# Layer 1 MLP: VectorE's low halves one item behind ScalarE's high halves, no weight items between two pairs of feature tiles

## The chip, the cores and the metric

The kernel runs on one core of one Trainium2 chip. The metric is the device time of one execution in microseconds (us); less is better. TensorE (PE) multiplies, VectorE (DVE) and ScalarE (ACT) work element by element, GpSimd (POOL) helps them, SyncE (SP) issues the DMA transfers. Each engine works through its own queue in program order and waits where an operand isn't ready.

## The reference, cut to what matters

Two layers of a diffusion backbone on 512 latent and 128 context tokens, with 1024 features, all in 32-bit floating point. Each layer ends with an MLP of 4096 hidden features:

```
def squared_relu_mlp(h, w1, w2):
    a = jax.nn.relu(h @ w1)
    return (a * a) @ w2

h = rms_norm(x, norm2_g[l]) * (1 + sc2) + sh2
x = x + g2 * squared_relu_mlp(h, w_ff1[l], w_ff2[l])
```

The change is in the MLP of layer 1, the last large stage before the final norm.

## The kernel before, in words

**High and low halves.** Every matrix operand is kept as two parts: a high half, the value rounded to TensorE's fast 32-bit format (fp32r), and a low half, the value minus its high half. One product is made of three matmuls (`mm3`, L805 to L810): high times high, high times low, low times high. The high half is written by ScalarE (a copy), the low half by VectorE (a subtraction that reads the high half). So the two engines hand each item on to each other.

**The weight queue.** `Weights` holds a list of items in the order of their use. `loads` (L176) issues their DMAs into five raw buffers of 128 x 1024 values, as far as these are free. `pump` (L195) processes the next item: ScalarE writes the high half (L216), VectorE the low half (L225), and `used` (L244) gives the raw buffer back, which lets the next load be issued. If no weight slot is free, `pump` does nothing. `need` (L255) pumps until an item is there. The calls of `pump` stand between the matmul groups and so fix the order of the work on ScalarE and VectorE. Some other items (the modulation's, L457) release code a counted number of items later (`flush`, L248).

**Up projection with seven products.** Layer 1's hidden features come in eight blocks of 512 (four feature tiles of 128). Blocks 0 and 1 are computed in the ordinary way ahead of `blocks7` (L1644). From block 2 on, `up7` (L1562) computes two feature tiles f and g for both token chunks of 320 (0 and 1) at once, with seven products instead of eight (a Strassen-like scheme). A block has two such pairs, p = 0 and 1. The seven weight operands of a pair (items `w1s`, 0 to 6) are combinations of four quarters f0, g0, f1, g1 of the raw weights. `w1s_use` (L555) writes the high half of an item (L565, 128 x 512), its low half (L566), and for items 0, 1, 2 and 4 a follow-up (L570) that overwrites a quarter in place; the follow-up of item 0 is read by item 1, that of 1 by 2, that of 2 by 3, that of 4 by 5.

Within a pair the products run in the order 0 to 6, each 12 matmuls. ScalarE copies the result of product 0 to p1 (L1615). VectorE makes u2 = p1 + product 2 and u3 = u2 + product 1 (L1620, L1621, traced at L1593 in `add`). Product 4 adds into the bank that product 1 left and u3 has read; products 5 and 6 likewise add into the banks of products 3 and 0. Sums with u2 and u3 give the hidden features of (g, 1), (g, 0) and (f, 1); (f, 0) comes straight from the last bank. `finish` (L1595) squares the positive part (ScalarE: Relu L1603, Square L1604; for (f, 0) Relu L1600 and a multiplication by VectorE, L1601), writes the high half (ScalarE, L1605) and returns the low half (VectorE, L1606), which is issued a product later.

**Down projection.** After a block's two pairs come its 16 down tiles (8 feature tiles x 2 chunks, 12 matmuls each), each followed by a residual update on VectorE (L1414) and, from the third tile on, one call of `pump`. The first four tiles start with half of their products. The four down weights of a block (items `w2`, 128 x 1024) are queued behind its 14 `w1s` items. Behind the last tile stands one `pump(2)` (L1670). So, in the steady state, the first pair's weights and item 0 of the second pair are processed in the down tiles, items 1 and 2 of the second pair between the blocks, items 3 to 6 and the first down weight in the first pair, the other three down weights in the second pair. While blocks 0 and 1 are multiplied down, VectorE and ScalarE also make the sums of activations that the seven products need (`sums`, L1516).

The last block (7) goes through its down tiles in two wider chunks of tokens (384 and 256), without any call of `pump`.

Of the kernel before, what the change touches and what calls it, by code (L numbers as in the profile page):

```python
# [136 lines left out]
class Weights:  # L137
# [3 lines left out]
    def __init__(self, nc, raw):  # L141
        self.nc, self.raw = nc, raw
        self.items, self.loaded, self.done = [], 0, 0
        self.raw_live, self.raw_cap, self.tiles, self.of = 0, RAWB, {}, {}
        self.raws = {}
        self.slots = None
        self.caps = {}

        self.lo = nc.vector
        self.own = {}  # L150
        self.hold = None
        self.slow = ()
        self.later, self.skip = [], False
        self.keep, self.second = {}, None

    def add(self, key, loads, size, use=None):
        self.items.append((key, loads, size, use))
# [37 lines left out]
    def pump(self, n=1):  # L195

        if self.skip:
            self.skip = False
            return
        while n > 0 and self.done < len(self.items):  # L200
            key, loads, size, use = self.items[self.done]
            own = self.own.get(key)
            if (use is None or key[0] == "w1s") and own is None and self.full(key) or key == self.hold:
                return
            self.loads()
            if self.done not in self.raws:
                return
            ts = self.raws.pop(self.done)
            if use is None:
                if own is None:  # L210
                    self.of[key], w = self.slots.take([128, 2, 1024], F32R)
                else:
                    w = own()
                r = ts[0][:, 0:size]
                hi, lo = w[:, 0, 0:size], w[:, 1, 0:size]
                self.nc.scalar.activation(out=hi, in_=r, func=AF.Copy)  # L216
                eng = self.nc.gpsimd if key[0] in self.slow else self.lo
                if eng is None:
                    self.nc.scalar.activation(out=lo, in_=hi.bitcast(F32), func=AF.Copy, scale=-1.0)
                    src, shape = loads[0]  # L220
                    if len(shape) == 2:
                        lo = lo.rearrange("p (k n) -> p k n", k=shape[0])
                    self.nc.gpsimd.dma_start(out=lo, in_=src, accum_op=ALU.add)
                else:
                    eng.tensor_tensor(out=lo, in0=r, in1=hi.bitcast(F32), op=ALU.subtract)  # L225
                self.tiles[key] = w
                rest = None
            else:
                rest = use(ts)
            self.done += 1  # L230
            for f in self.later:
                f[0] -= 1
            self.flush(0)
            if rest:

                self.skip = False
                d = self.done
                self.pump()
                rest()
                self.skip = self.done > d  # L240
            self.used(self.keep.pop(key, len(loads)))
            n -= 1

    def used(self, n):  # L244
        self.raw_live -= n
# [9 lines left out]
    def need(self, key):  # L255
        while key not in self.tiles:
            self.skip = False
            d = self.done
            self.pump(1)
            assert self.done > d, (key, self.items[self.done][0])  # L260
        return self.tiles[key]

    def free(self, key):
# [12 lines left out]
def body(ctx, tc, a):  # L276
# [278 lines left out]
    def w1s_use(l, b, p, i):  # L555


        def use(ts):
            if i == 0:
                fast[l, b, p] = ts  # L560
            ab, cd = (t.rearrange("p (k n) -> p k n", k=4) for t in fast[l, b, p])
            f0, g0, f1, g1 = ab[:, :, 0:128], ab[:, :, 128:256], cd[:, :, 0:128], cd[:, :, 128:256]
            src = (f0, g0, g0, f0, g1, g0, f1)[i]
            w = st.half(("w1s", l, b, p, i)).rearrange("p a (k n) -> p a k n", k=4)
            act(out=w[:, 0], in_=src, func=AF.Copy)  # L565
            vec.tensor_tensor(out=w[:, 1], in0=src, in1=w[:, 0].bitcast(F32), op=ALU.subtract)  # L566
            todo = {0: (g0, f0, g0, ALU.subtract), 1: (g0, g1, g0, ALU.subtract), 2: (f0, g0, f0, ALU.add),
                    4: (g0, f1, g0, ALU.subtract)}.get(i)
            if todo:
                vec.tensor_tensor(out=todo[0], in0=todo[1], in1=todo[2], op=todo[3])  # L570

        return use

# [880 lines left out]
    def mlp(l, C, H, lead, CL, per_d, per_c, mid, tick=None, turn=None, seven=False):  # L1454
# [107 lines left out]
        def up7(b, p):  # L1562
            n = C[0][1]

            gone = []

            def product(i, op, ps, first):
                w = st.need(("w1s", l, b, p, i))
                if ps is None:
                    ps = bank("up_ps", n)  # L1570
                for k in range(4):
                    r = B[op, k] if isinstance(op, int) else H[op[0]][4 * op[1] + k]
                    mm3(
                        ps, (w[:, 0, tok(k)], w[:, 1, tok(k)]), (r[:, 0, 0:n], r[:, 1, 0:n]),
                        first and k == 0, k == 3, not first,
                    )

                gone.append(("w1s", l, b, p, i))
                if i:
                    st.free(gone.pop(0))  # L1580
                return ps

            f, g = 2 * p, 2 * p + 1
            rs = {}
            for j in (f, g):
                A[b, j] = fa.tile([128, 2, T], F32R, tag="aa", name="aa")
                rs[j] = fr.tile([128, 2, HW], F32, tag="r", name="r").rearrange("p a n -> p (a n)")

            def new(nm):
                return sc.tile([128, 328], F32, tag="n", name=nm)[:, 0:n]  # L1590

            def add(out, v, ps):
                vec.tensor_tensor(out=out, in0=v, in1=ps, op=ALU.add)  # L1593

            def finish(j, ci, src=None):  # L1595

                c = slice(*C[ci])
                r, aa = rs[j][:, c], A[b, j]
                if src is not None:
                    act(out=r, in_=src, func=AF.Relu)  # L1600
                    vec.tensor_tensor(out=r, in0=r, in1=src, op=ALU.mult)  # L1601
                else:
                    act(out=r, in_=r, func=AF.Relu)  # L1603
                    act(out=r, in_=r, func=AF.Square)  # L1604
                act(out=aa[:, 0, c], in_=r, func=AF.Copy)  # L1605
                return lambda: vec.tensor_tensor(  # L1606
                    out=aa[:, 1, c], in0=r, in1=aa[:, 0, c].bitcast(F32), op=ALU.subtract
                )

            def out(j, ci):  # L1610
                return rs[j][:, C[ci][0]:C[ci][1]]

            pa = product(0, (0, 0), None, True)
            p1 = new("p1")
            act(out=p1, in_=pa, func=AF.Copy)  # L1615
            st.pump()
            pd = product(1, 2, None, True)
            pb = product(2, 1, None, True)
            u2, u3 = new("u2"), new("u3")
            add(u2, p1, pb)  # L1620
            add(u3, u2, pd)  # L1621
            st.pump()
            pc = product(3, 0, None, True)
            add(out(g, 1), u3, pc)
            lo = finish(g, 1)
            st.pump()
            pd = product(4, 3, pd, False)
            add(out(g, 0), u2, pd)
            lo()
            lo = finish(g, 0)  # L1630
            if not p:
                st.pump()
            pc = product(5, (1, 1), pc, False)
            add(out(f, 1), u2, pc)
            lo()
            lo = finish(f, 1)
            if not p:
                st.pump()
            pa = product(6, (0, 1), pa, False)
            lo()  # L1640
            finish(f, 0, pa)()
            st.free(gone.pop(0))

        def blocks7(f0):  # L1644

            for b in range(NFB):
                if b >= f0:
                    for p in range(FB // 2):
# [7 lines left out]
                if b < NFB - 1:  # L1656
# [10 lines left out]
                    free(1)  # L1667
                    if b == f0 - 1:
                        bg.drain()
                    st.pump(2)  # L1670
                    continue
                for c in CL:
                    early = cut(range(3), CL[0:1]) if c is CL[0] else []
                    for d in range(KD):
                        if d < len(early):
                            ps = down(b, d, c, early[d][2], True, (3, 2))
                        else:
                            ps = down(b, d, c)
                        residual(ps, d, c, modc[l, 5])
                        per_d(c, d)  # L1680
                    per_c(c)
# [522 lines left out]
```

## Time and profile before

| what | before |
|---|---|
| time, median of 3 runs | 1323.13 us (1322.59 to 1324.24) |
| the profiled execution | 1321.14 us |
| its span, first to last instruction | 1319.2 us |
| mean granted TensorE clock | 0.978 |
| instructions | 20782 |
| busy: PE, DVE, ACT, POOL | 96%, 62%, 42%, 16% of the span |
| HBM read, written | 144.21 MB, 5.39 MB |

The page of the profile gives the busy time of each engine and the costliest groups of instructions. The view of waits says which instruction stood still for which other one. The timeline gives the instructions of an engine with their start and length, and in brackets the idle time before one and what ended it. The view of windows gives busy times and the granted TensorE clock in chosen stretches. "Low" and "high" are used below for the two halves of an item, "follow-up" for the subtraction at L570.

### The profile page before, as it was taken

The page shows a single profiled execution, that of the slowest core. Times are in us where ns is not written, and L with a number is a line of the kernel's source. Part 1 is how long each engine was busy: PE and PEld are TensorE (multiplying, and loading weights), DVE is VectorE, ACT ScalarE, POOL GpSimd, SP SyncE. Part 2 cuts the span into 40 slices and gives each one's busy share as a digit, 9 for nine tenths or more (in the row PEclk, how much of TensorE's full clock was granted, in tenths as well). Part 3 has the DMA queues.
Part 4 walks back from the last instruction along what each step waited for, and adds up shares of the span by engine and source line. Part 5 has one row for each costly group of instructions (what it writes and reads, how often), then busy time and mean ns, then how long its engine had stood idle before and what let it go on. Part 6 is the DMA issues. An engine that isn't in the chain of part 4 may idle for free.

```text
span 1319.2 us, 20782 instructions
## 1 busy us (share of the span) xinstructions
PE 1266.0 (96%) x8308; PEld 1193.5 (90%) x8308; DVE 823.2 (62%) x1565; ACT 551.4 (42%) x989; POOL 206.7 (16%) x182
## 2 busy tenths in 40 slices
PE   7999999999999999999999999899989898998987
PEld 5899875689999999999999998889989898998987
DVE  5753864554766666665666546767867566565654
ACT  3445454543553434333343425543242434334243
POOL 0010322212022222222222233300000000000001
PEclk8999899999999999999999998999989999999999
DMA  7742297250344444444343606503121312222102
GB/s 279 264 163 77 80 231 252 97 192 1 130 129 144 128 160 123 149 128 141 119 157 123 214 17 145 111 17 111 34 88 41 96 49 80 81 80 89 40 32 80
DMA packets 65376, 154.09 MB, mean 117 GB/s; under 512 B 5200, under 2 KB 22096, under 8 KB 64768
## 3 DMA queue, kind: packets, MB, share of 16 engines
q1 hardware_dynamic: 61360, 142.53, 32.9%
q0 software_dynamic: 3632, 10.16, 3.7%
q8 instruction: 65, 1.06, 0.3%
q14 instruction: 31, 0.25, 0.1%
q10 hardware_dynamic: 288, 0.08, 0.0%
HBM read 144.21 MB, written 5.39 MB: 113 GB/s over the span
## 4 chain that ended last, share of the span: by engine, by line
PE 75%; DVE 14%; ACT 7%; issue 2%; DMA 1%; POOL 0%; DVEq 0%; ACTq 0%; POOLq 0%
PE dn_ps L809 10%; PE dn_ps L808 10%; PE dn_ps L810 10%; PE up_ps L808 8%; PE up_ps L810 7%; PE up_ps L809 7%; ACT w L216 2%; DVE w L225 2%; DVE w L566 2%; DVE x L1414 2%; PE o_ps L1309 1%; PE wo_ps L808 1%; PE wo_ps L809 1%; PE wo_ps L810 1%; PE mod_ps L351 1%
## 5 line engine op out<-in xcount | busy, mean ns | idle before, releaser
L808 PE MATMUL dn_ps<-aa,w 128*128 128x320 f32 (+4 forms) x1024 | 317.8, 310 | 0.0
L809 PE MATMUL dn_ps<-aa,w 128*128 128x320 f32 (+4 forms) x1024 | 317.2, 310 | 0.0
L810 PE MATMUL dn_ps<-aa,w 128*128 128x320 f32 (+4 forms) x1024 | 316.4, 309 | 0.0
L809 PE MATMUL up_ps<-h,w 128*128 128x320 f32 (+2 forms) x800 | 249.0, 311 | 4.6 <-DVE h L759 4.6
L808 PE MATMUL up_ps<-h,w 128*128 128x320 f32 (+2 forms) x800 | 251.0, 314 | 1.3 <-ACT h L755 1.3
L810 PE MATMUL up_ps<-h,w 128*128 128x320 f32 (+2 forms) x800 | 249.4, 312 | 0.0
L1414 DVE SCALAR_TENSOR_TENSOR x<-dn_ps,mod,x 128x328 f32<-128x328 f32 (+5 forms) x360 | 145.0, 434 | 114.5 <-PE dn_ps L810 113.6
L225 DVE TENSOR_TENSOR w<-raw,w 128x1024 fp32r<-128x1024 f32 (+4 forms) x122 | 151.8, 1250 | 86.5 <-ACT w L216 85.4
L808 PEld LDWEIGHTS dn_ps<-aa,w 128*128 128x128 f32 x1024 | 192.6, 188 | 1.8 <-issue 0.8
L809 PEld LDWEIGHTS dn_ps<-aa,w 128*128 128x128 f32 x1024 | 192.5, 188 | 0.1
L810 PEld LDWEIGHTS dn_ps<-aa,w 128*128 128x128 f32 x1024 | 192.6, 188 | 0.0
L216 ACT ACTIVATE w<-raw 128x1024 fp32r<-128x1024 f32 (+4 forms) x131 | 132.7, 1026 | 114.1 <-DMA raw<-w_ff 86.9
L809 PEld LDWEIGHTS up_ps<-h,w 128*128 128x128 f32 x800 | 152.4, 191 | 5.4 <-DVE h L759 5.4
L808 PEld LDWEIGHTS up_ps<-h,w 128*128 128x128 f32 x800 | 152.7, 191 | 4.9 <-issue 3.4
L810 PEld LDWEIGHTS up_ps<-h,w 128*128 128x128 f32 x800 | 151.8, 190 | 0.0
L473 POOL TENSOR_TENSOR acc<-acc,raw 128x1024 f32<-128x1024 f32 x42 | 100.7, 2399 | 303.7 <-ACT raw L471 297.6
L565 ACT ACTIVATE w<-raw 128x512 fp32r<-128x512 f32 x84 | 50.9, 624 | 120.7 <-DVE raw L570 70.1
L566 DVE TENSOR_TENSOR w<-raw,w 128x512 fp32r<-128x512 f32 x84 | 57.8, 688 | 40.2 <-ACT w L565 39.6
L471 ACT ACTIVATE raw<-raw,cs 128x1024 f32<-128x1024 f32 x42 | 48.3, 1149 | 62.3 <-DVE acc L466 53.9
L1942 POOL TENSOR_TENSOR y<-y,fg 128x1024 f32<-128x1024 f32 x1 | 2.4, 2389 | 439.4 <-ACT y L1938 439.4
L1488 DVE TENSOR_TENSOR r<-r,up_ps 128x328 f32<-128x328 f32 (+2 forms) x80 | 37.4, 484 | 41.3 <-ACT r L1487 39.7
L1491 DVE TENSOR_TENSOR aa<-r,aa 128x640 fp32r<-128x640 f32 (+3 forms) x52 | 39.8, 766 | 35.6 <-ACT aa L1490 35.6
(407 smaller groups left out, 2134.3 us busy)
## 6 DMA issues: line engine op xcount, KB each, us to landing
raw<-w_ff SPq DMA_DIRECT2D x126, 512.0 KB, 3.7
raw<-w_mod SPq DMA_DIRECT2D x80, 512.0 KB, 3.9
raw<-w_m SPq DMA_DIRECT2D x16, 512.0 KB, 6.2
raw<-w_out SPq DMA_DIRECT2D x8, 512.0 KB, 4.3
w<-w_ff POOLq DMA_DIRECT2D x8, 512.0 KB, 10.0
kT<-ckvT POOLq DMA_DIRECT2D x4, 768.0 KB, 11.1
xr<-x SPq DMA_DIRECT2D x5, 512.0 KB, 5.6
xs<-x SPq DMA_DIRECT2D x2, 1280.0 KB, 8.9
```

The costliest lines, as they stand in the source:

```text
L216: self.nc.scalar.activation(out=hi, in_=r, func=AF.Copy)
L225: eng.tensor_tensor(out=lo, in0=r, in1=hi.bitcast(F32), op=ALU.subtract)
L471: act(out=raw if k else acc[1], in_=raw, func=AF.Copy, scale=w[1])
L473: nc.gpsimd.tensor_tensor(out=acc[1], in0=acc[1], in1=raw, op=ALU.add)
L565: act(out=w[:, 0], in_=src, func=AF.Copy)
L566: vec.tensor_tensor(out=w[:, 1], in0=src, in1=w[:, 0].bitcast(F32), op=ALU.subtract)
L808: mm(ps, lhsT=st_[0], rhs=mv[0], start=first, stop=False, skip_group_check=on)
L809: mm(ps, lhsT=st_[0], rhs=mv[1], start=False, stop=False, skip_group_check=on)
L810: mm(ps, lhsT=st_[1], rhs=mv[0], start=False, stop=last, skip_group_check=on)
L1414: vec.scalar_tensor_tensor(out=xv, in0=ps[:, p0:p0 + c1 - c0], scalar=gate[:, d, m:m + 1], in1=xv, op0=ALU.mult, op1=ALU.add)
L1488: vec.tensor_tensor(out=rv, in0=rv, in1=ps, op=ALU.mult)
L1491: vec.tensor_tensor(out=aa[:, 1, lo:hi], in0=r[:, lo:hi], in1=aa[:, 0, lo:hi].bitcast(F32), op=ALU.subtract)
```

## The change

There are four edits.

1. `Weights` gets a list `lag` and a flag `lagging`. The low half of an item (for `w1s` with its follow-up) and the return of its raw buffer are put on the list instead of being issued at once. Without the flag the list is emptied at the end of the same item; with the flag (set at the start of `blocks7`) it is emptied when the next item is about to be processed, or when the item itself is needed. In both cases the released code of `flush` now stands ahead of the low half.
2. In `up7` the first call of `pump` moves from behind product 0 to behind product 1, and the one behind product 4 is now made in both pairs.
3. `finish` becomes `high` (Relu, Square and the high half, all on ScalarE, also for (f, 0)) and `low`. The sum of a chunk is issued ahead of the high half of the chunk before it, and the low halves come one product later or at the end of the pair.
4. The `pump(2)` behind a block's down tiles is taken out, and the last block's down tiles get one call of `pump` each.

```
     def pump(self, n=1):
...
         while n > 0 and self.done < len(self.items):
+            self.lows()
             key, loads, size, use = self.items[self.done]
...
-                    eng.tensor_tensor(out=lo, in0=r, in1=hi.bitcast(F32), op=ALU.subtract)
+                    self.lag.append(
+                        lambda: eng.tensor_tensor(out=lo, in0=r, in1=hi.bitcast(F32), op=ALU.subtract)
+                    )
...
-            self.used(self.keep.pop(key, len(loads)))
+            n_raw = self.keep.pop(key, len(loads))
+            self.lag.append(lambda: self.used(n_raw))
+            if not self.lagging:
+                self.lows()
             n -= 1
+
+    def lows(self):
+
+        todo, self.lag = self.lag, []
+        for f in todo:
+            f()
...
     def need(self, key):
...
+            self.lows()
+        if self.lag and key == self.items[self.done - 1][0]:
+            self.lows()
         return self.tiles[key]
...
             act(out=w[:, 0], in_=src, func=AF.Copy)
-            vec.tensor_tensor(out=w[:, 1], in0=src, in1=w[:, 0].bitcast(F32), op=ALU.subtract)
             todo = {0: (g0, f0, g0, ALU.subtract), 1: (g0, g1, g0, ALU.subtract), 2: (f0, g0, f0, ALU.add),
                     4: (g0, f1, g0, ALU.subtract)}.get(i)
-            if todo:
-                vec.tensor_tensor(out=todo[0], in0=todo[1], in1=todo[2], op=todo[3])
+
+            def lows():
+                vec.tensor_tensor(out=w[:, 1], in0=src, in1=w[:, 0].bitcast(F32), op=ALU.subtract)
+                if todo:
+                    vec.tensor_tensor(out=todo[0], in0=todo[1], in1=todo[2], op=todo[3])
+
+            st.lag.append(lows)
...
-            def finish(j, ci, src=None):
-
+            def high(j, ci, src=None):
                 c = slice(*C[ci])
-                r, aa = rs[j][:, c], A[b, j]
-                if src is not None:
-                    act(out=r, in_=src, func=AF.Relu)
-                    vec.tensor_tensor(out=r, in0=r, in1=src, op=ALU.mult)
-                else:
-                    act(out=r, in_=r, func=AF.Relu)
-                    act(out=r, in_=r, func=AF.Square)
-                act(out=aa[:, 0, c], in_=r, func=AF.Copy)
-                return lambda: vec.tensor_tensor(
-                    out=aa[:, 1, c], in0=r, in1=aa[:, 0, c].bitcast(F32), op=ALU.subtract
-                )
+                r = rs[j][:, c]
+                act(out=r, in_=r if src is None else src, func=AF.Relu)
+                act(out=r, in_=r, func=AF.Square)
+                act(out=A[b, j][:, 0, c], in_=r, func=AF.Copy)
+
+            def low(j, ci):
+                c = slice(*C[ci])
+                hi, lo = (A[b, j][:, i, c] for i in range(2))
+                vec.tensor_tensor(out=lo, in0=rs[j][:, c], in1=hi.bitcast(F32), op=ALU.subtract)
...
             act(out=p1, in_=pa, func=AF.Copy)
+            pd = product(1, 2, None, True)
             st.pump()
-            pd = product(1, 2, None, True)
             pb = product(2, 1, None, True)
...
             pc = product(3, 0, None, True)
             add(out(g, 1), u3, pc)
-            lo = finish(g, 1)
             st.pump()
             pd = product(4, 3, pd, False)
             add(out(g, 0), u2, pd)
-            lo()
-            lo = finish(g, 0)
-            if not p:
-                st.pump()
+            high(g, 1)
+            st.pump()
             pc = product(5, (1, 1), pc, False)
+            low(g, 1)
             add(out(f, 1), u2, pc)
-            lo()
-            lo = finish(f, 1)
+            high(g, 0)
             if not p:
                 st.pump()
             pa = product(6, (0, 1), pa, False)
-            lo()
-            finish(f, 0, pa)()
+            low(g, 0)
+            high(f, 1)
+            high(f, 0, pa)
+            low(f, 1)
+            low(f, 0)
...
         def blocks7(f0):
 
+            st.lagging = True
             for b in range(NFB):
...
                         bg.drain()
-                    st.pump(2)
                     continue
...
                             ps = down(b, d, c)
+                        st.pump()
                         residual(ps, d, c, modc[l, 5])
                         per_d(c, d)
```

More of the change, by code (lines that the diff above doesn't have):

```diff
@@ L154, in __init__ @@
         self.keep, self.second = {}, None
+        self.lag, self.lagging = [], False
     def add(self, key, loads, size, use=None):
```

## The prediction

> **What bounds the kernel now.** I read the page first.
>
> ```profile
> span 1319.2 us, 20782 instructions
> ...
> PE 1266.0 (96%) x8308; PEld 1193.5 (90%) x8308; DVE 823.2 (62%) x1565; ACT 551.4 (42%) x989; POOL 206.7 (16%) x182
> ```
>
> TensorE works nearly all the time, so only what makes it stand still or run slowly is worth anything. The change acts from the layer 1 blocks on (about 898 us to 1282 us), so next came the view of waits from 925 to 1285 us.
>
> ```profile
> ACT w L565 <- DVE raw L570: 70.1, 33, 4.7
> ...
> DVE w L566 <- ACT w L565: 39.6, 45, 2.1
> DVE x L1414 <- PE dn_ps L810: 35.9, 51, 1.2
> DVE w L225 <- ACT w L216: 32.2, 18, 2.5
> PE up_ps L808 <- DVE u L1593: 23.2, 7, 4.0
> ```
>
> Columns: total us, times, longest. The last row is the only one that costs time: TensorE waits seven times for the sums u2 and u3. The others show why VectorE is late: it waits for ScalarE's copies and ScalarE for VectorE's results, in turn, each with little of its own queued meanwhile.
>
> Two rows of TensorE's timeline place the wait: always the fifth product (index 4) of a block's second pair, because it adds into the bank that u3 must first have read.
>
> ```profile
> 1038.71 0.51 PE L808 MATMUL up_ps<-w 128*128 128x320 f32 x1 [3.49 <-DVE u L1593]
> ...
> 1096.78 0.56 PE L808 MATMUL up_ps<-w 128*128 128x320 f32 x1 [3.49 <-DVE u L1593]
> ```
>
> They are 58.07 us apart, one block. The view of windows shows a second price behind such a wait (columns: window, length, busy us and instructions of PE, PEld, DVE, ACT, POOL, granted clock, DMA share, GB/s).
>
> ```profile
> 1020.00:1023.00 3.00, 3.00 (x22) 3.00 (x21) 2.39 (x5) 1.06 (x2) 0.00 (x0) 1.00 0.00 0
> ...
> 1038.70:1041.95 3.25, 3.24 (x12) 3.25 (x13) 1.40 (x2) 1.75 (x4) 0.00 (x0) 0.52 0.78 214
> ...
> 982.20:985.00 2.80, 2.80 (x19) 2.80 (x20) 1.37 (x2) 1.34 (x4) 0.00 (x0) 1.00 0.73 206
> ```
>
> After the 3.49 us wait the clock is 0.52 for 3.25 us: 3.25 x 0.48 = 1.56 us lost. The window at 982.20 follows the shortest of the seven waits (in the first layer-1 block of the seven-product form) and has clock 1.00. That wait is 23.2 - 4.0 - 5 x 3.49 = 1.7 us long.
>
> **What can be won.** The rows below are VectorE's timeline, from the end of one block through the next one's first pair into its second.
>
> ```profile
> 1012.36 0.68 DVE L1414 SCALAR_TENSOR_TENSOR x<-dn_ps,mod,x 128x192 f32<-128x192 f32 x2 [1.21 <-PE dn_ps L810]
> 1014.12 0.55 DVE L1414 SCALAR_TENSOR_TENSOR x<-dn_ps,mod,x 128x320 f32<-128x320 f32 x1 [1.08 <-PE dn_ps L810]
> 1015.88 0.68 DVE L1414 SCALAR_TENSOR_TENSOR x<-dn_ps,mod,x 128x192 f32<-128x192 f32 x2 [1.21 <-PE dn_ps L810]
> ...
> 1022.10 0.68 DVE L566 TENSOR_TENSOR w<-raw,w 128x512 fp32r<-128x512 f32 x1
> 1022.70 0.68 DVE L570 TENSOR_TENSOR raw<-raw 128x512 f32<-128x512 f32 x1
> ...
> 1034.13 0.48 DVE L1601 TENSOR_TENSOR r<-r,up_ps 128x320 f32<-128x320 f32 x1
> 1035.15 0.49 DVE L1606 TENSOR_TENSOR aa<-r,aa 128x320 fp32r<-128x320 f32 x1 [0.54 <-ACT aa L1605]
> 1036.42 1.23 DVE L225 TENSOR_TENSOR w<-raw,w 128x1024 fp32r<-128x1024 f32 x1 [0.78 <-ACT w L216]
> 1037.57 0.48 DVE L1593 TENSOR_TENSOR u<-p,up_ps 128x320 f32<-128x320 f32 x1
> 1038.08 0.49 DVE L1593 TENSOR_TENSOR u<-u,up_ps 128x320 f32<-128x320 f32 x1
> 1038.48 1.22 DVE L225 TENSOR_TENSOR w<-raw,w 128x1024 fp32r<-128x1024 f32 x1
> ```
>
> Each residual waits for TensorE, so 12 matmuls (one product, one down tile) take 1.76 us. A block is 14 products and 16 down tiles: 30 x 1.76 = 52.8 us. It takes 58.07, so 5.27 us are lost: the 3.49, the 1.56 and some 0.2 of pipeline refill. Five blocks: 5 x 5.27 = 26.4. The first block of the form loses 4.0 + 1.7 + 1.56 + 2 x 0.2 = 7.7. Together 34.1 us: all that this change can win.
>
> **Moving the lows and the adds: the new schedule of a pair.** ScalarE's rows for the same stretch:
>
> ```profile
> 1017.92 0.63 ACT L565 ACTIVATE w<-raw 128x512 fp32r<-128x512 f32 x1 [2.28 <-DVE raw L570]
> 1018.45 0.42 ACT L1615 ACTIVATE p<-up_ps 128x320 f32<-128x320 f32 x1
> ...
> 1030.63 0.47 ACT L1604 ACTIVATE r<-r 128x320 f32<-128x320 f32 x1
> 1031.14 0.47 ACT L1605 ACTIVATE aa<-r 128x320 fp32r<-128x320 f32 x1
> 1031.51 1.04 ACT L216 ACTIVATE w<-raw 128x1024 fp32r<-128x1024 f32 x1
> 1032.46 0.41 ACT L1600 ACTIVATE r<-up_ps 128x320 f32<-128x320 f32 x1
> 1034.65 0.47 ACT L1605 ACTIVATE aa<-r 128x320 fp32r<-128x320 f32 x1 [1.77 <-DVE r L1601]
> 1035.03 0.42 ACT L1615 ACTIVATE p<-up_ps 128x320 f32<-128x320 f32 x1
> 1035.34 1.99 ACT L216 ACTIVATE w<-raw 128x1024 fp32r<-128x1024 f32 x2
> ```
>
> Paces read from both fences: on VectorE the next instruction starts 0.60 us after a 512-wide one, 0.40 after a 320-wide one, 0.51 if it needs the one before; on ScalarE a 512-wide high takes 0.53 to the next start, three dependent 320-wide steps 1.48 in all; a hand-over between the engines costs 0.03 to 0.04 (1034.61 to 1034.65, 1035.12 to 1035.15). Zero is the last residual's start (1015.88), so product k of the first pair is readable at 1.76(k+1). TensorE wants product 4 of the second pair at 11 x 1.76 less the 0.2 by which it runs ahead of readers: 19.16. Before, u3 ended at 1038.57, which is 22.69; 3.5 late, as the waits say, so the clock of this sum is right.
>
> Following the new program order (the first pair now processes weight items 1 to 5 of the second, none in the gap before it):
> - VectorE does u2 at 5.28, u3 at 5.79, the low of item 1 at 6.19, its follow-up (L570) at 6.79, ending 7.48.
> - The high of item 2 reads that follow-up: ScalarE 7.52 to 8.14. VectorE fills the time with the add of (g,1), 7.39 to 7.87. The low of item 2 runs from 8.17, its follow-up ends at 9.46.
> - High 3 9.50 to 10.12; add (g,0) 9.37 to 9.85; low 3 from 10.15. ScalarE's three steps for (g,1) run 10.03 to 11.52, high 4 to 12.04.
> - VectorE: low (g,1) 11.55, add (f,1) 11.95, low of item 4 12.35, follow-up to 13.64. ScalarE: (g,0) 11.95 to 13.43, high 5 13.68 to 14.30, (f,1) to 15.69, (f,0) 15.59 to 17.03 with Square in place of VectorE's multiplication at L1601.
> - VectorE: low (f,1) 15.72, low (f,0) 17.06 to 17.55. ScalarE copies p1 of the second pair 16.94 to 17.36.
> - Second pair: low of item 5 at 17.46, u2 18.06, u3 18.58 to 19.07. TensorE, released 0.14 later (1038.57 to 1038.71), starts at 19.21 instead of 19.16.
>
> So the wait falls from 3.5 to about 0.1 us a block, 0.6 us in six blocks, and the slow clock goes with it. The gain comes from no low standing behind a ScalarE copy of the same item just ahead of u2, and from one item fewer before them. From 19.07 on, the same paces give the last low of the pair at about 27.3; the down tiles read it from about 28 on. That 0.8 us is its cover; without it, each 0.1 us late costs 0.1 a block.
>
> **The rest of the edits.** In the down tiles each step costs VectorE a residual (0.55 to 0.68), a low and at most a follow-up (1.2), against TensorE's 1.76, and six banks cover a short queue: nothing. Buffers come free one item later, so SyncE issues later.
>
> ```profile
> raw<-w_ff SPq DMA_DIRECT2D x41, 512.0 KB, 3.7
> ```
>
> A load lands 3.7 us after issue. The closest one, the next block's first weights, is issued at about 21.4 and 23 on the clock above and used at about 31.7: hidden twice over. In the first block of the form the waits for ScalarE that are taken out let VectorE catch up before the first pair; I take its waits as gone too, with up to 4 us (its present one) as the other end. In the last block the fourth down weight now gets its low only when the fifth tile asks for it.
>
> ```profile
> 1286.39 0.62 DVE L1414 SCALAR_TENSOR_TENSOR x<-dn_ps,mod,x 128x384 f32<-128x384 f32 x1 [1.46 <-PE dn_ps L810]
> 1288.48 0.62 DVE L1414 SCALAR_TENSOR_TENSOR x<-dn_ps,mod,x 128x384 f32<-128x384 f32 x1 [1.47 <-PE dn_ps L810]
> ```
>
> It follows a residual (0.54) with 1.22 us, while TensorE has 8 of 12 matmuls (1.39 of 2.09) to do: a wait of about 0.5, between 0 and 1.1. In layer 0 the helper now emits a low behind the code that the counter releases:
>
> ```profile
> L488 DVE COPY modrow<-mod_ps x6: 684/692/693, 428.1 to 747.6; 128x512 f32<-128x512 f32 x6
> its engine sat idle before it (us, times) until:
>   PE mod_ps L483: 13.5, 4
> ```
>
> In four of six cases a low of 1.22 us that filled this wait moves behind it. TensorE waits for nothing of VectorE's there; I take 0, and at most 4 x 1.22 = 4.9. A gain there is excluded: nothing becomes earlier.
>
> Sum: 34.1 - 0.6 - 0.5 = 33.0. The profiled execution took 1321.14 us (span 1319.2), so 1288.1; the median of the runs lies 2.0 above it (1323.13): **1290 us**.
>
> **The rivals.**
> 1. *The chain stays serial.* Highs 2, 3 and 5 still wait for the follow-up before them, which now is issued just ahead of them; anything my hand schedule leaves out lands on u3. For it speaks the 70.1 us in 33 waits, 2.1 each, where high 3 waits 1.4 in my schedule (8.14 to 9.50). Three times the 0.7 of difference is 2.1 us: a wait of about 2.1 a block remains. It is near the 1.7 us wait behind which the clock stayed at 1.00, so the clock's share is still won: 34.1 - 6 x 2.1 - 0.5 = 21.0, about 1302 us. Between 1.7 and 3.49 the rows don't say where the clock falls. [...]
> 2. *Slower: ScalarE is held up by VectorE.* Behind each of highs 2, 3 and 5 now stand the squares of the pair and p1. If each waited 4.7 us, the longest in the row, instead of 1.4, u3 would be 9.9 us later, 6.3 later than before: 6 x 6.3 = 38 us, about 1361. It turns slower from an average of 2.6 us per wait (three times 1.2 makes up the 3.6 by which u3 comes earlier). Against it: in the pair VectorE has only one add queued ahead of these items, and the long waits stand in the down tiles, behind residuals.
> 3. *No effect.* The lag is there only where a later item is processed; if the wait simply moved to another product, 34 us would stay lost: 1320 to 1325. Against it: every other operand of the second pair is ready 2 us or more early in the schedule above (item 1 ends at 7.5 and is wanted at 13.9, item 5 at 18.1, wanted at 20.9).
>
> **How the numbers follow.** My forecast (waits left of up to 0.6 us a block) has 0.62: 1287 to 1297. Rival 1, with waits of 0.6 to 3 us, 0.22: 1294 to 1308. Rival 2 0.06, rival 3 0.05, something between 1308 and 1320 0.05. All 34.1 won is 1289; the lower end, 1286, lies 3 us below that for the spread of the runs shown (1322.59 to 1324.24) and what the 0.2 of refill may hide. The upper end, 1306, takes in most of rival 1 and the unknown costs of the other edits (4.9, 4 and 1.1). 0.2% (2.6 us) is about what a measurement of this kernel can tell from no change. Faster 0.89, same 0.04, slower 0.07.
>
> **What would show it.** Right: the row of TensorE waiting for u at the add's line falls from 23.2 us to under 4; blocks repeat every 52.8 to 53.5 us; the granted clock in the blocks is 1.00; the multiplication by the bank is gone from VectorE and 48 Square steps stand on ScalarE. ScalarE's wait for the follow-up may well grow: that alone proves nothing. Wrong: TensorE waits of over 1 us in the second pair, a clock of 0.5 behind them, a new wait at the first down tiles for a low of the activations, or ScalarE waiting for a weight load.

## The result and the profile after

| | before | after |
|---|---|---|
| median of 4 runs each, same chip | 1323.68 us (1322.59 to 1325.63) | 1289.74 us (1287.65 to 1293.12) |
| profiled execution | 1321.14 us | 1291.31 us |
| mean granted TensorE clock | 0.978 | 0.987 |

The ratio is 0.974, with a 95% interval of 0.972 to 0.977: faster by 33.9 us in the medians. The page of the changed kernel:

```profile
span 1289.5 us, 20770 instructions
...
PE 1256.4 (97%) x8308; PEld 1184.2 (92%) x8308; DVE 816.4 (63%) x1553; ACT 554.9 (43%) x1001; POOL 206.4 (16%) x182
...
PEclk8999999999999999999999999889999999999998
```

TensorE does the same 8308 matmuls; 12 instructions have gone from VectorE and 12 have come to ScalarE (the squares of the (f, 0) chunks). A slice is 32.2 us; from 870 us on, the clock is at 9 (90% or more) in every slice but the last.

The view of waits, from 925 to 1285 us, as in the prediction:

```profile
ACT w L581 <- DVE raw L588: 108.5, 42, 7.9
...
DVE w L586 <- ACT w L581: 5.2, 17, 0.4
ACT r L1618 <- DVE r L1613: 2.0, 6, 0.3
PE up_ps L828 <- DVE u L1613: 1.1, 6, 0.2
```

TensorE's wait for u, 23.2 us in 7 before, is 1.1 us in 6. VectorE's wait for the copies of the weights fell from 39.6 to 5.2 us. ScalarE's wait for the follow-ups (the first row) grew from 70.1 to 108.5 us, as the prediction said it might, and TensorE waits for none of these highs. One row of the kernel before that the prediction didn't show is the counterpart of the third one here:

```profile
ACT r L1603 <- DVE r L1593: 57.4, 30, 2.8
```

ScalarE's three steps waited 57.4 us for VectorE's sums before, and wait 2.0 now. The first experiments explain this row.

TensorE's timeline at product 4 of the second pair in two blocks that follow each other, and in the last block's down tiles:

```profile
1028.81 0.38 PE L828 MATMUL up_ps<-w 128*128 128x320 f32 x1 [0.18 <-DVE u L1613]
...
1082.06 0.38 PE L828 MATMUL up_ps<-w 128*128 128x320 f32 x1 [0.20 <-DVE u L1613]
...
1257.47 0.44 PE L830 MATMUL dn_ps<-aa,w 128*128 128x384 f32 x1 [0.45 <-DVE w L228]
```

A block now takes 53.25 us (58.07 before). The wait stands at the same product and is 0.2 us idle; from start to start it is 0.48 us against the usual 0.147, so it costs 0.34 at this matmul. The last row is the low of the fourth down weight. The window over the whole stretch (columns as in the prediction):

```profile
970.00:1280.00 310.00, 308.43 (x2101) 306.61 (x2099) 202.20 (x400) 137.00 (x272) 4.91 (x3) 1.00 0.23 75
```

The clock is 1.00 throughout, and TensorE is busy for 308.43 of 310 us.

Whole executions differ by some microseconds ahead of the change's stage: the first layer 1 down matmul comes at 899.5 us in this trace and at 894.1 us in a second one of the same kernel. So below, the time from the first layer 1 down matmul to the last is used beside the medians, and called the stage. It took 411.7 us before (898.1 to 1309.8) and 380.3 us after (899.5 to 1279.8): 31.4 us less. In the second trace of the kernel after it is 380.3 again.

### The profile page after: what moved, and what is told of

Same layout as the page of the kernel before. It is cut to its first block, busy times and chain, and to the rows that moved or that the text cites. A ratio compares the mean times of both kernels' runs of the same rounds, so it can differ in the third digit from the quotient of the medians.

```text
span 1289.5 us, 20770 instructions
## 1 busy us (share of the span) xinstructions
PE 1256.4 (97%) x8308; PEld 1184.2 (92%) x8308; DVE 816.4 (63%) x1553; ACT 554.9 (43%) x1001; POOL 206.4 (16%) x182
## 3 DMA queue, kind: packets, MB, share of 16 engines
q1 hardware_dynamic: 61360, 142.53, 33.9%
## 4 chain that ended last, share of the span: by engine, by line
PE 83%; DVE 8%; ACT 5%; DMA 2%; issue 1%; POOL 0%; DVEq 0%; ACTq 0%; POOLq 0%
PE dn_ps L829 12%; PE dn_ps L828 12%; PE dn_ps L830 12%; PE up_ps L828 9%; PE up_ps L830 9%; PE up_ps L829 9%; PE o_ps L1329 1%; PE wo_ps L828 1%; PE wo_ps L829 1%; PE wo_ps L830 1%; DVE w L586 1%; PE t_ps L1296 1%; PE mod_ps L367 1%; DMA raw<-w_mod 1%; PE s_ps L828 1%
## 5 line engine op out<-in xcount | busy, mean ns | idle before, releaser
L581 ACT ACTIVATE w<-raw 128x512 fp32r<-128x512 f32 x84 | 51.0, 625 | 108.5 <-DVE raw L588 108.5
L1511 DVE TENSOR_TENSOR aa<-r,aa 128x640 fp32r<-128x640 f32 (+3 forms) x52 | 39.6, 762 | 35.6 <-ACT aa L1510 35.6
```

The lines of the kernel that those rows point to most:

```text
L1511: vec.tensor_tensor(out=aa[:, 1, lo:hi], in0=r[:, lo:hi], in1=aa[:, 0, lo:hi].bitcast(F32), op=ALU.subtract)
```

## The experiments

**What was to be told apart.** Theory A: what the change breaks is a loop between the engines. VectorE's sum of one chunk releases ScalarE's three steps; behind these stands the high half of a weight; behind that, on VectorE, its low half; and behind the low half the next sum. Two edits cut this loop independently: the lag of the weights' lows (edit 1), and the new order of sums and steps (edit 3). Either should do, and the new places of the pump calls (edits 2 and 4) alone should not. Rivals: the places do it (one item fewer ahead of u2, none between the pairs), or both cuts are needed together. Theories A and B in a quoted expectation are that expectation's own.

**Lag alone** (edit 1; the old `finish`, the old places, `pump(2)` back).

```
-            def high(j, ci, src=None): ...   def low(j, ci): ...
+            def finish(j, ci, src=None): ...
...
+                    st.pump(2)
```

> Only the lag of the weights' low halves (edit 1); pump positions, finish and the pump behind the down tiles as before. Theory A (either of the two lags is enough, since each takes the waiting lows out of the way ahead of u2): by the paces of the trace u3 ends at about 18.6 on the clock of the prediction, before TensorE wants it (19.16); no wait for u is left, the clock stays at 1.00, about 1289 us (1286 to 1294). Theory B (the three edits are needed together): a wait of over 1.5 us a block stays, 1300 to 1315 us.

Measured: 1288.28 us (1286.89 to 1289.78), ratio 0.975 (0.973 to 0.978). Its stage is 377.9 us. No product waits for u in any block; only the last block's down tile still waits for its low (0.45 us idle, 0.65 from start to start more than usual). From 970 to 1272 us TensorE is busy for 301.55 of 302.00 us. The sums of one first pair start at 1015.55, 1017.31 and 1019.08 us on VectorE: 1.76 us apart, the pace of TensorE's products.

**Places alone** (edits 2 and 4, with the old `finish` and without the lag).

```
-            st.lagging = True
...
+            lo = finish(g, 1)
             st.pump()
             pd = product(4, 3, pd, False)
             add(out(g, 0), u2, pd)
+            lo()
+            lo = finish(g, 0)
             st.pump()
```

> Only the places of the pump calls change (edits 2 and 4); lows and finish as before. Theory A: the wait for u shrinks from 3.5 to about 2.5 us a block, and since the last lows of the pair come later (about 2.3 us after the first down tiles want them), a wait of that size appears there; both below the length at which the clock fell, so 30 us of waits in place of 34 of waits and slow clock: 1312 to 1322 us. Theory B (the order of the weight items is the main thing): under 1300 us.

Measured: 1323.21 us (1318.81 to 1327.87), ratio 1.002 (1.000 to 1.004): no gain. Its stage is 413.2 us, 1.5 more than before. The view of waits of this kernel, from 925 to 1285 us:

```profile
ACT r L1623 <- DVE r L1613: 68.7, 36, 3.1
...
DVE w L586 <- ACT w L581: 53.7, 50, 2.1
...
PE up_ps L828 <- DVE u L1613: 14.2, 7, 2.6
...
PE dn_ps L828 <- ACT aa L1625: 4.2, 5, 1.9
```

The waits for u are shorter than before (14.2 against 23.2 us), but the first two rows, the two halves of the loop, are as large as before or larger, and the down tiles now wait for the activations. One turn of the loop, first on ScalarE and then on VectorE of this kernel:

```profile
1026.08 0.47 ACT L1623 ACTIVATE r<-r 128x320 f32<-128x320 f32 x1 [1.16 <-DVE r L1613]
1026.58 0.47 ACT L1624 ACTIVATE r<-r 128x320 f32<-128x320 f32 x1
1027.08 0.47 ACT L1625 ACTIVATE aa<-r 128x320 fp32r<-128x320 f32 x1
1027.46 0.62 ACT L581 ACTIVATE w<-raw 128x512 fp32r<-128x512 f32 x1
1029.84 0.47 ACT L1623 ACTIVATE r<-r 128x320 f32<-128x320 f32 x1 [1.76 <-DVE r L1613]
```

```profile
1025.57 0.48 DVE L1613 TENSOR_TENSOR r<-u,up_ps 128x320 f32<-128x320 f32 x1
1025.96 0.49 DVE L1626 TENSOR_TENSOR aa<-r,aa 128x320 fp32r<-128x320 f32 x1
1028.11 0.69 DVE L586 TENSOR_TENSOR w<-raw,w 128x512 fp32r<-128x512 f32 x1 [1.66 <-ACT w L581]
1028.72 0.68 DVE L588 TENSOR_TENSOR raw<-raw 128x512 f32<-128x512 f32 x1
1029.32 0.48 DVE L1613 TENSOR_TENSOR r<-u,up_ps 128x320 f32<-128x320 f32 x1
```

Read it as one line: sum at 1025.57, 0.51 later Relu, 1.38 for the three steps, 0.65 for the high half, 0.61 for the low, 0.60 for the follow-up, and the next sum at 1029.32. That is 3.75 us a turn, in which ScalarE idles 1.76 and VectorE 1.66, while TensorE hands over a product every 1.76. Neither engine is short of time; they only take turns. Where the item has no follow-up, the turn is shorter by it. So it is in the kernel before, on VectorE:

```profile
1026.46 0.48 DVE L1593 TENSOR_TENSOR r<-u,up_ps 128x320 f32<-128x320 f32 x1
1026.86 0.49 DVE L1606 TENSOR_TENSOR aa<-r,aa 128x320 fp32r<-128x320 f32 x1
1029.01 0.69 DVE L566 TENSOR_TENSOR w<-raw,w 128x512 fp32r<-128x512 f32 x1 [1.66 <-ACT w L565]
1029.62 0.48 DVE L1593 TENSOR_TENSOR r<-u,up_ps 128x320 f32<-128x320 f32 x1
```

These two sums are 3.16 us apart, and the sum before them starts another 3.16 us earlier, at 1023.30: still far above 1.76.

**The new order of sums and steps alone** (edit 3; no lag, old places, `pump(2)` back).

```
-            st.lagging = True
...
             add(out(g, 0), u2, pd)
             high(g, 1)
-            st.pump()
+            if not p:
+                st.pump()
...
+                    st.pump(2)
```

> Only the squares and lows of the activations change (edit 3, with Square on ScalarE for all four); pump places and the weights' lows as before. Theory A: u3 at about 18.6, no wait for u left, 1287 to 1294 us. Theory B: a wait of over 1.5 us a block stays, 1300 to 1315 us.

Measured: 1293.23 us (1289.02 to 1294.07), ratio 0.979 (0.976 to 0.981). The stage is 383.7 us. From the second pair of the first seven-product block on no product waits, and the sums of one first pair start at 1017.02, 1018.50 and 1020.79, at most 2.29 us apart. All that is left is a wait in the first pair, in TensorE's timeline:

```profile
961.13 0.63 PE L828 MATMUL up_ps<-w 128*128 128x320 f32 x1 [4.08 <-DVE u L1613]
```

That is the wait of 4.0 us that the kernel before has at the same place, and the clock is halved behind it too (0.51 from 961.00 to 966.50 us). Blocks 0 and 1 stand ahead of it, and edit 3 does not touch them.

**Everything without the lag** (edits 2, 3 and 4).

```
-            st.lagging = True
```

> The whole change without the lag of the weights' lows (the flag is never set). Theory A: u3 at about 18.6, no wait for u left, the last low of the activations 3.4 us after the pair's last product, just inside the cover; 1287 to 1293 us. Theory B (the lag carries the gain): a wait of over 1.5 us a block comes back, 1300 us or more.

Measured: 1287.49 us (1285.94 to 1290.12), ratio 0.975 (0.972 to 0.978); stage 379.5 us. Only the first seven-product block still waits, 1.23 and 0.72 us.

What follows from these four: Theory A holds. Lag alone and order alone each take out the waits of all later blocks, places alone win no time, and the two cuts together are not needed. Only the first block separates them: there order alone leaves 4.08 us, the places without the lag leave 1.23 and 0.72, and the lag alone leaves nothing. Edit 3 also moves the multiplication for (f, 0) to ScalarE; which part of that edit cuts the loop was not tried, and lag alone wins with the multiplication still on VectorE. The medians of lag alone, of everything without the lag and of the kernel after lie within 2.3 us, less than the runs of the kernel after differ among themselves (5.5).

**The 0.34 us that are left.** In the kernel after, a low still stands ahead of u2. VectorE's timeline of that kernel:

```profile
1014.64 0.49 DVE L1613 TENSOR_TENSOR u<-p,up_ps 128x320 f32<-128x320 f32 x1 [4.67 <-PE up_ps L830]
1015.16 0.49 DVE L1613 TENSOR_TENSOR u<-u,up_ps 128x320 f32<-128x320 f32 x1
1015.57 0.69 DVE L586 TENSOR_TENSOR w<-raw,w 128x512 fp32r<-128x512 f32 x1
1016.29 0.69 DVE L588 TENSOR_TENSOR raw<-raw 128x512 f32<-128x512 f32 x1
...
1026.65 0.49 DVE L1625 TENSOR_TENSOR aa<-r,aa 128x320 fp32r<-128x320 f32 x1 [0.84 <-ACT aa L1620]
1027.06 0.69 DVE L586 TENSOR_TENSOR w<-raw,w 128x512 fp32r<-128x512 f32 x1
1027.66 0.48 DVE L1613 TENSOR_TENSOR u<-p,up_ps 128x320 f32<-128x320 f32 x1
1028.18 0.49 DVE L1613 TENSOR_TENSOR u<-u,up_ps 128x320 f32<-128x320 f32 x1
```

The low at 1027.06 is that of item 5, issued by the second pair's first `pump`. Four kernels were compared: the kernel after once more; the same with that `pump` moved behind u2 and u3; the same with `pump(2)` back between the blocks; and lag alone with the last block's low repaired.

The kernel after again:

> The changed kernel once more, as the yardstick of this call: a wait for u of about 0.2 us (0.34 from start to start) in each of six blocks and one of 0.65 in the last block's fifth down tile, by its profile; 1287 to 1293 us.

Measured: 1285.71 us (1284.34 to 1290.19), ratio 0.974 (0.972 to 0.976), stage 380.3: six times 0.34 and once 0.65 as before.

The pump moved behind the sums, and lows released in the last block:

```
             pd = product(1, 2, None, True)
-            st.pump()
+            if not p:
+                st.pump()
...
             add(u3, u2, pd)
-            st.pump()
+            st.pump(1 + p)
...
     def pump(self, n=1):
+        if self.done == len(self.items):
+            self.lows()
```

> The changed kernel with the second pair's first pump call moved from behind product 1 to behind u2 and u3 (two items there), and the last weight's low half issued behind the last block's first down tile. Theory A (the 0.34 us left a block is the low half of item 5 just ahead of u2): u3 about 0.5 earlier, no wait left, 2.7 us under the changed kernel. Theory B (it is the hand-overs between the engines): the 0.34 stays.

Measured: 1285.04 us (1282.27 to 1288.95), ratio 0.973 (0.971 to 0.976), stage 377.0. The window from 970 us to the end of the stage, and VectorE's timeline around u2:

```profile
970.00:1274.00 304.00, 304.00 (x2082) 303.76 (x2080) 200.83 (x399) 134.44 (x268) 5.11 (x4) 1.00 0.23 77
```

```profile
1023.64 0.48 DVE L1615 TENSOR_TENSOR u<-p,up_ps 128x320 f32<-128x320 f32 x1
1024.15 0.49 DVE L1615 TENSOR_TENSOR u<-u,up_ps 128x320 f32<-128x320 f32 x1
1024.56 1.29 DVE L588 TENSOR_TENSOR w<-raw,w 128x512 fp32r<-128x512 f32 x2
```

The lows of items 5 and 6 now follow u3, and TensorE is busy for 304.00 of 304.00 us. So the 0.34 was that low. A block takes 52.82 us here against 53.24 in the kernel after: a wait costs 0.42 in all, 0.34 at its own matmul and 0.08 at the next one, which starts 0.22 us later in place of 0.147.

`pump(2)` back, all else as in the kernel after:

```
                         bg.drain()
+                    st.pump(2)
                     continue
```

> The changed kernel with the two items between the blocks put back. Theory A (with the lag they do no harm, as they fall in the 4.7 us in which VectorE has nothing to do ahead of the first u2): u3 0.2 earlier, no wait for u or at most 0.1 a block, 0 to 2 us under the changed kernel. Theory B (the items between the blocks make VectorE late): a wait of over 1 us a block, 1296 us or more.

Measured: 1286.97 us (1283.27 to 1288.26), ratio 0.974 (0.972 to 0.976), stage 377.8. No product waits for u, only the last block's 0.65 stays. So keeping weights out of the gap between the pairs is not needed for the gain. It costs the wait in each block, because it leaves item 5 to the place ahead of u2.

Lag alone, with the last block's pumps and the release above:

```
+        if self.done == len(self.items):
+            self.lows()
...
                             ps = down(b, d, c)
+                        st.pump()
```

> Edit 1 alone, and the low half of the last weight is issued behind the first down tile of the last block in place of the fifth. Theory A (VectorE's lateness is the only thing that the blocks lose, and the lag alone takes it away): no wait for u, no wait for a weight in the last block, blocks of 52.8 us; 2.7 us under the changed kernel (6 x 0.34 + 0.65). Theory B (the other edits carry something that the waits don't show): as fast as the changed kernel or slower.

Measured: 1285.17 us (1282.78 to 1289.26), ratio 0.973 (0.971 to 0.976), stage 377.1: no wait of TensorE is left in the stage. So edit 1 with one repair gives all there was to win. The medians of these four kernels lie within 2 us and inside each other's ranges; it is the stage that orders them.

**Where the clock falls.** Places alone left waits of about 2.2 us with the half clock behind most of them (0.51 in the 3.41 us from 1036.80 and in those from 1094.83), where rival 1 of the prediction had counted on the clock being full. In the traces of the kernels before and after, the granted clock changes only at times a whole multiple of 3.413 us apart: in the one before at 963.72, 970.54, 1038.81, 1042.22 and 1096.84 us, which is 2, 20, 1 and 16 times that. A window in the next two expectations is such a stretch of 3.413 us, 0.5 and 1.00 are granted clocks, and a fall is one from 1.00 to 0.5. Two kernels gave the second pair of each block a wait of another length: additions into u2 and u3, which the real sums then overwrite, so nothing is left out of the computation.

```
             u2, u3 = new("u2"), new("u3")
+            for i in range(b + 2 if p else 0):
+                add((u2, u3)[i % 2], p1, p1)
```

> The changed kernel with idle additions of 320 columns (0.40 us each, results overwritten) on VectorE ahead of u2 in each second pair: 4, 5, 6, 7, 8 and 9 of them in blocks 2 to 7. TensorE's idle time before product 4 should climb from about 1.8 to 3.8 us in steps of 0.4 (if additions that overwrite each other are paced at 0.51, from 2.2 to 4.8). [...] Theory B (a share of a window is enough, as the 2.2 us waits of the kernel with only the pump places changed suggest): 0.5 from the wait of about 2.2 us on. Each wait costs its length, each fall another 1.6 us.

And the same with `11 - b` additions:

> The same with 9, 8, 7, 6, 5 and 4 additions in blocks 2 to 7, so that waits of the same length meet other positions of the clock's window. [...] Theory B: 0.5 down to the wait of about 2.2 us, 1.00 at 1.8.

Measured, one execution each: 1311.80 and 1311.42 us. The waits of the first were 1.81, 2.38, 2.62, 3.19, 3.39 and 4.00 us; the granted clock behind the first five was 0.50, 1.00, 0.50, 1.00 and 0.50. Those of the other were 4.00, 3.40, 3.21, 2.60, 2.38 and 1.79 us; behind the one of 3.21 us, which ended at 1092.59, the matmuls start 0.27 us apart up to 1096.09 and 0.147 from there on. Three waits of the first kernel in TensorE's timeline, and the windows that follow them:

```profile
973.84 0.38 PE L828 MATMUL up_ps<-w 128*128 128x320 f32 x1 [1.81 <-DVE u L1613]
...
1030.80 0.38 PE L828 MATMUL up_ps<-w 128*128 128x320 f32 x1 [2.38 <-DVE u L1613]
...
1144.23 0.38 PE L828 MATMUL up_ps<-w 128*128 128x320 f32 x1 [3.19 <-DVE u L1613]
```

```profile
975.30:978.70 3.40, 3.40 (x15) 3.40 (x14) 2.56 (x4) 3.12 (x6) 0.00 (x0) 0.50 0.77 223
1030.80:1034.20 3.40, 3.40 (x23) 3.40 (x24) 3.36 (x5) 2.45 (x5) 0.00 (x0) 1.00 0.48 148
1144.20:1147.60 3.40, 3.37 (x23) 3.40 (x24) 3.36 (x5) 2.42 (x5) 0.00 (x0) 1.00 0.50 139
```

A wait of 1.81 us halved the clock and one of 3.19 us did not. So theory B holds in its first half alone: a share of a stretch was enough, but it is no fixed length of the wait. What fits these waits is their place. Counted in steps of 3.413 us from the fall at 975.30, the wait of 1.81 us (972.03 to 973.84) lies wholly in one such stretch; the one of 3.19 us (1141.04 to 1144.23) is cut by the edge at 975.30 + 49 x 3.413 = 1142.54 into 1.50 and 1.69; the one of 2.38 us by the edge at 1029.91 into 1.49 and 0.89. Two waits of almost the same length in the kernel with the places alone show it side by side, in TensorE's timeline and in the windows behind:

```profile
1036.50 0.38 PE L828 MATMUL up_ps<-w 128*128 128x320 f32 x1 [2.17 <-DVE u L1613]
...
1209.20 0.39 PE L828 MATMUL up_ps<-w 128*128 128x320 f32 x1 [2.16 <-DVE u L1613]
```

```profile
1036.80:1040.20 3.40, 3.40 (x15) 3.40 (x14) 1.09 (x2) 2.21 (x4) 0.00 (x0) 0.50 0.83 234
1209.20:1212.60 3.40, 3.40 (x23) 3.40 (x24) 1.39 (x2) 1.91 (x4) 0.00 (x0) 1.00 0.75 211
```

The first lies in one stretch (1033.39 to 1036.80), the second is cut into 0.42 and 1.74 (TensorE busy for 2.99 of the 3.41 us from 1204.05 and for 1.68 of the 3.42 from 1207.46).

## Why the prediction was right, and where not

**The bound and the price of the waits: right.** The stage of the kernel with no wait left takes 377.0 us against 411.7 before: 34.7 us to be won, where the prediction had 34.1 from the period of the blocks. The 0.6 more lies in the first block. The windows of the kernel before, in and behind its wait of 4.0 us (961.61 to 965.65):

```profile
960.30:963.70 3.40, 1.31 (x9) 1.04 (x8) 2.20 (x4) 1.33 (x3) 0.00 (x0) 1.00 0.00 0
963.75:967.10 3.35, 1.45 (x5) 1.46 (x6) 3.08 (x6) 0.72 (x2) 0.00 (x0) 0.50 0.02 5
967.15:970.50 3.35, 3.35 (x14) 3.35 (x14) 1.23 (x4) 2.00 (x5) 0.00 (x0) 0.50 0.00 0
```

The clock was halved for two stretches, not one, in which TensorE was busy for 4.8 us: 2.4 us were lost where the sum has 1.56.

**The schedule by hand: right but for a quarter of a microsecond.** u2 of the first pair started at 1014.64, which the schedule puts at 5.28, so its zero is at 1009.36. The low of item 1 then started at 6.21 (forecast 6.19), its follow-up at 6.93 (6.79), the low of item 5 at 17.70 (17.46), u2 at 18.30 (18.06), and u3 ended at 19.31 (19.07). Half of the slip of 0.24 is the first follow-up, which started 0.72 us behind its low (1015.57 to 1016.29) where the sum used 0.60. So a wait costs 0.42 us instead of 0.1 (the 0.08 behind it is in no term of the sum), six times: 2.5 instead of 0.6. This is the mis-sized term.

**The last block: right in kind.** 0.65 us at the matmul that waits and 0.8 in the stage (377.9 for lag alone, 377.1 with the repair), forecast 0.5 between 0 and 1.1. **The first block:** its waits went, as taken. **Layer 0:** VectorE's wait at the released code grew as foreseen, from 13.5 to 18.9 us, and TensorE waits for nothing of VectorE's there:

```profile
L504 DVE COPY modrow<-mod_ps 128x512 f32<-128x512 f32 x6 | 4.1, 690 | 18.9 <-PE mod_ps L499 18.9
```

**The sum.** 33.0 us were forecast for the stage and 31.4 came. By the terms as measured it is 34.7 - 2.5 - 0.8 = 31.4: the waits took 2.2 us more than their terms, and 0.6 more was there to be won. The medians differ by 33.9 us because whole executions also vary ahead of the stage; that the median fell on the forecast to 0.3 us is partly luck.

**The reason: half right.** The prediction gave two: no low waiting for its copy just ahead of u2, and one item fewer before the sums. The second is wrong: places alone brought nothing, and with the two items back in the gap the stage was 2.5 us shorter. The first names only the last link. The loop runs through the first pair, in turns of 3.16 us (3.75 with a follow-up), and u2 is merely where its delay reaches TensorE. The prediction read the waits "in turn" but laid out only the new schedule. A schedule of the old order, with one edit at a time, would have shown that either edit alone is enough; the expectations of lag alone and of the new order alone have it, with u3 at about 18.6.

**Rival 1** (the chain stays serial, the clock won back) did not come, but places alone is such a case, and its price was wrong. Its waits were about 2.2 us, seven stretches of 3.41 us in its stage ran at a clock of 0.50 (7 x 1.7 = 11.9 us), and no time was gained. The kernel before has as many: two at its first wait and one behind each of the five of 3.49 us. The 1.7 us wait with full clock in the kernel before, on which that price rested, had been cut by an edge at 980.78 into 0.34 and 1.40. That price went by the lengths of two waits; the first of the windows above had already shown a fall behind 2.1 us of idle time (busy for 1.31 of 3.40 us). That waits of up to 3 us leave the clock full, as its range of 1294 to 1308 us has it, no run shows: the clock was 0.50 behind waits of 1.81, 2.17 and 2.62 us. **Rival 2** did not come: in the pair, high 3 waited 1.42 us for its follow-up (forecast 1.4), and the longest such waits, 7.85 us, stand in the down tiles, where nothing waits for them. **Rival 3** is what places alone did.

## What to carry to other kernels

Where two engines hand each item on to each other and both show long waits with little work, write one turn of the loop as a sum of hand-overs and compare it with the pace of the engine that they feed; here 3.16 to 3.75 us against 1.76. One cut is enough, and it is an instruction issued one item later, so that an engine never queues the reader of a result right behind the request for it. Test the edits of such a change one by one: the bundle of four was no faster than its first edit with one repair, and one of its edits, no weights in the gap, cost 2.5 us of the stage.

## What the runs showed of the hardware

The granted TensorE clock changed only on a grid of 3.413 us, which ran on through all waits between: in the kernel before it fell, among other times, at 158.17, 963.72, 1038.81, 1096.84 and 1270.92 us, which is 236, 22, 17 and 51 such stretches apart; in the kernel after at 156.14, 818.33 and 1282.54 us, 194 and 136 apart. In the stage, every measured stretch with 1.81 us or more of idle time was followed by a stretch at half clock (0.50 over 3.413 us: 1.7 us lost); the 1.81 was seen twice, ahead of 975.30 in the first of the two kernels with additions and, in places alone, in the stretch from 1217.70 (TensorE busy for 1.61 of 3.42 us, clock 0.51 behind). A stretch with 1.74 us, from 1207.46 in places alone, had a clock of 1.00 behind it. So waits of 1.81 to 3.19 us cost 1.7 us more or nothing, as the edges happened to fall: 2.17 us halved the clock, 2.16 did not. This limit, a bit over half of a stretch (1.81 of 3.413), is one of the stage alone. Where it ends, in the kernel after, TensorE was busy for 1.81 of the 3.41 us from 1279.12 (1.60 idle), and the clock was 0.50 behind; ahead of it, in the kernel before, for 2.67 of the 3.40 us from 810.12, and the clock was 0.50 behind that too. What else decides there, no run shows.
